# Channel shuffle in place: eight buffers of 24 KB a partition, or four of 48 KB

## The chip, the cores and the metric

One core of a Trainium2 chip. The metric is the device time of one execution in microseconds: 317.66 us before the change, the median of three runs (317.65 to 317.87). A profiled execution gives the trace that is read here.

## The reference

The tensor x has 16 x 64 x 64 positions of 256 channels in float32. The channels of each position are read as 8 groups of 32 and written in the order 32 times 8: a transpose of an 8 x 32 block within each position.

```python
x = x.reshape(batch, h, w, groups, channels_per_group)
x = x.transpose(0, 1, 2, 4, 3)
x = x.reshape(batch, h, w, c)
```

Nothing is computed; 67.1 MB are read and 67.1 MB are written.

## The kernel before, in words

The 65,536 positions (rows of 1 KB) are cut into tiles of 128 x q rows. `_SIZES` (line 12) lists q for each tile: twenty tiles of 24, one of 8, one of 24. Each partition holds q consecutive rows, so a tile with q = 24 is 24 KB a partition and 3 MB in all, and both its load and its store move one contiguous run of 24 KB a partition.

For each tile in turn (line 48), a buffer is taken from a pool of eight (line 49), one DMA loads the tile on SP's queue (line 50), and then pieces of 8 rows (1 MB, 8 KB a partition) are shuffled: VectorE (DVE) copies the piece into one of two PSUM buffers named bounce, reading it with the 8 and 32 exchanged (line 54), and ScalarE (ACT) copies it back to where it came from (line 58). After its last piece the tile is stored by one DMA on ACT's queue (line 59). A buffer is free for its next load when its store has landed.

The order of the work is the order in which the program is written: `manual_schedule` keeps each engine's instructions in that order, so a store on ACT that has to wait also holds the copies that ACT does behind it, and with two bounce buffers DVE stops two pieces later. All DMAs, loads and stores together, use eight semaphores in turn; a DMA is not issued before the last DMA that used its semaphore has landed.

Of the kernel before, what the change touches and what calls it, by code (L numbers as in the profile page):

```python
# [1 line left out]

# [4 lines left out]


F32 = mybir.dt.float32
P = 128  # L10

_SIZES = [24] * 20 + [8, 24]
_BUFS = 8

_PIECE = 8


@with_exitstack
def kernel(
    ctx: ExitStack,  # L20
    tc: tile.TileContext,
    x: bass.AP,
    groups: bass.AP,
    out: bass.AP,
):
    nc = tc.nc
    b, h, w, c = x.shape
    G = int(groups)
    CPG = c // G
    assert G * CPG == c  # L30
    assert sum(_SIZES) * P == b * h * w
    biggest = max(_SIZES)

    x_flat = x.rearrange("b h w c -> (b h w c)")
    out_flat = out.rearrange("b h w c -> (b h w c)")

    pool = ctx.enter_context(tc.tile_pool(name="pool", bufs=_BUFS))
    psum = ctx.enter_context(
        tc.tile_pool(name="psum", bufs=2, space=bass.MemoryType.PSUM)
    )  # L40

    def rows(flat, first, q):

        return flat[first * c : (first + P * q) * c].rearrange("(p f) -> p f", p=P)

    ctx.enter_context(tc.manual_schedule(engines=None))
    first = 0
    for q in _SIZES:
        buf = pool.tile([P, biggest * c], F32, name="buf")
        nc.sync.dma_start(out=buf[:, : q * c], in_=rows(x_flat, first, q))  # L50
        for k in range(0, q, _PIECE):
            piece = buf[:, k * c : (k + _PIECE) * c]
            bounce = psum.tile([P, _PIECE * c], F32, name="bounce")
            nc.vector.tensor_copy(  # L54
                out=bounce.rearrange("p (i j g) -> p i j g", j=CPG, g=G),
                in_=piece.rearrange("p (i g j) -> p i j g", g=G, j=CPG),
            )
            nc.scalar.copy(out=piece, in_=bounce)  # L58
        nc.scalar.dma_start(out=rows(out_flat, first, q), in_=buf[:, : q * c])  # L59
        first += P * q  # L60


# [1 line left out]
_INS = ['x', 'groups']  # L64
_OUTS = [((16, 64, 64, 256), 'float32')]

_NUMBERS = {'groups': 8}


# [26 lines left out]
```

## Time and profile before

| | |
|---|---|
| median of three runs | 317.66 us |
| the profiled execution's own time | 317.64 us |
| its span | 315.9 us |
| DVE, 64 copies | 227.9 us busy, 3636 ns each |
| ACT, 64 copies back | 119.0 us busy, 1866 ns each |
| load of 3 MB, median from issue to landing | 58.4 us |
| store of 3 MB, median from issue to landing | 24.2 us |
| HBM read and written | 67.11 MB each, 425 GB/s over the span |

Times from issue to landing hold the time that a DMA stands in the queue behind others. The rows of the profile name an instruction by its line, engine, operation and tiles. Times in the timeline and in the chain of waits are microseconds from the start of the span. "DMA share" is the busy share of the 16 DMA engines, on which the queues of SP (q1) and ACT (q10) both run.

### The profile page before, as it was taken

To read this page: it belongs to the slowest core of one execution; us is meant where nothing else is said; L and a number is where in the kernel's file an instruction comes from. 1 tells how busy PE (TensorE), PEld (TensorE's weight loads), DVE (VectorE), ACT (ScalarE), POOL (GpSimd) and SP (SyncE) were. 2 spreads that over 40 slices of the span, in tenths; PEclk is the share of its full clock that TensorE was granted. 3 is DMA by queue.
4 is the path that set the end of the run, shared out by engine and by line. 5 is a ranking of instruction groups with operands and counts; after the bars stand their busy time and mean duration, and the time that the engine had idled before them with its cause. 6 is when DMAs were issued, how large, how long until landed. Compare 5 with 4: busy or idle time off the path is not lost.

```text
span 315.9 us, 289 instructions
## 1 busy us (share of the span) xinstructions
DVE 227.9 (72%) x64; ACT 120.3 (38%) x65; POOL 0.2 (0%) x4
## 2 busy tenths in 40 slices
DVE  0699999959587685957008986999970299999900
ACT  0354455525252424330015416545500444555420
POOL 0000000000000000000000000000000000000000
DMA  8999999999999999999999999999999999999997
GB/s 296 439 442 380 436 429 433 433 439 433 423 442 433 426 442 426 426 442 426 433 436 427 433 436 436 433 426 437 433 423 448 423 429 444 429 423 433 439 432 302
DMA packets 6338, 134.24 MB, mean 425 GB/s; under 512 B 704, under 2 KB 704, under 8 KB 704
## 3 DMA queue, kind: packets, MB, share of 16 engines
q1 hardware_dynamic: 3168, 67.11, 49.9%
q10 hardware_dynamic: 3168, 67.11, 49.4%
q14 instruction: 2, 0.02, 0.0%
HBM read 67.11 MB, written 67.11 MB: 425 GB/s over the span
## 4 chain that ended last, share of the span: by engine, by line
DVE 54%; another core or an unknown queue 23%; issue 8%; ACT 5%; DMA 3%; DVEq 1%; ACTq 0%
DVE bounce L54 54%; ACT buf L58 5%; DMA buf<-in_x_dram 3%; DVEq L91 1%; ACTq L59 0%; DVEq L54 0%; ACTq L58 0%
## 5 line engine op out<-in xcount | busy, mean ns | idle before, releaser
L54 DVE COPY bounce<-buf 128x2048 f32<-128x2048 f32 x64 | 227.9, 3636 | 72.6 <-ACT buf L58 38.8
L58 ACT COPY buf<-bounce 128x2048 f32<-128x2048 f32 x64 | 119.0, 1866 | 171.1 <-DVE bounce L54 115.3
L58 ACT ACT_TABLE_LOAD x1 | 1.3, 1283 | 11.1 <-DMA buf<-in_x_dram 11.1
L77 POOL MEMSET const-bfloat16-1.0<- 128x1 bf16 x1 | 0.1, 102 | 0.0
L77 POOL MEMSET const-uint8-127<- 128x1 uint8 x1 | 0.1, 101 | 0.0
L77 POOL MEMSET const-float32-0.0<- 128x1 f32 x1 | 0.1, 99 | 0.2 <-issue 0.2
L77 POOL MEMSET const-float32-1.0<- 128x1 f32 x1 | 0.1, 98 | 0.0
## 6 DMA issues: line engine op xcount, KB each, us to landing
buf<-in_x_dram SPq DMA_DIRECT2D x21, 3072.0 KB, 58.4
out_dram<-buf ACTq DMA_DIRECT2D x21, 3072.0 KB, 24.2
buf<-in_x_dram SPq DMA_DIRECT2D x1, 1024.0 KB, 46.0
out_dram<-buf ACTq DMA_DIRECT2D x1, 1024.0 KB, 15.8
```

The lines of the kernel that those rows point to most:

```text
L54: nc.vector.tensor_copy(out=bounce.rearrange("p (i j g) -> p i j g", j=CPG, g=G), in_=piece.rearrange("p (i g j) -> p i j g", g=G, j=CPG),)
L58: nc.scalar.copy(out=piece, in_=bounce)
L77: nc = _bacc.Bacc("TRN2", target_bir_lowering=False, num_devices=1)
L91: with _tile.TileContext(nc) as tc:
```

## The change

The tiles become one of 8, one of 24 and ten of 48, in this order, and the pool has four buffers of 48 KB a partition, as much memory as eight of 24 KB. A tile of 48 is loaded by two DMAs of 24 KB a partition each, both issued before its shuffle. Its pieces are shuffled as before, the first half's first. It is stored by one DMA of 48 KB a partition after its last piece; the last three tiles are stored by two DMAs, each half after its own third piece. Seven tiles of 48 are thus stored whole.

```diff
-_SIZES = [24] * 20 + [8, 24]
-_BUFS = 8
+_SIZES = [8, 24] + [48] * 10
+_BUFS = 4
+
+_LOAD = 24
+
+_HALVED = 3
...
-    for q in _SIZES:
+    for t, q in enumerate(_SIZES):
         buf = pool.tile([P, biggest * c], F32, name="buf")
-        nc.sync.dma_start(out=buf[:, : q * c], in_=rows(x_flat, first, q))
-        for k in range(0, q, _PIECE):
-            piece = buf[:, k * c : (k + _PIECE) * c]
...
-            nc.scalar.copy(out=piece, in_=bounce)
-        nc.scalar.dma_start(out=rows(out_flat, first, q), in_=buf[:, : q * c])
+        src, dst = rows(x_flat, first, q), rows(out_flat, first, q)
+        whole = t < len(_SIZES) - _HALVED
+        for a in range(0, q, _LOAD):
+            cols = slice(a * c, min(a + _LOAD, q) * c)
+            nc.sync.dma_start(out=buf[:, cols], in_=src[:, cols])
+        for a in range(0, q, _LOAD):
+            b = min(a + _LOAD, q)
+            for k in range(a, b, _PIECE):
+                piece = buf[:, k * c : (k + _PIECE) * c]
...
+                nc.scalar.copy(out=piece, in_=bounce)
+            if whole and b == q:
+                nc.scalar.dma_start(out=dst, in_=buf[:, : q * c])
+            elif not whole:
+                cols = slice(a * c, b * c)
+                nc.scalar.dma_start(out=dst[:, cols], in_=buf[:, cols])
         first += P * q
```

Below, tiles are counted from 0, and "a" and "b" are the first and second half of a tile of 48 (tile 9's second half is 9b).

More of the change, by code (lines that the diff above doesn't have):

```diff
@@ L26 @@
     nc = tc.nc
-    b, h, w, c = x.shape
+    n, h, w, c = x.shape
     G = int(groups)
@@ L30 @@
     assert G * CPG == c
-    assert sum(_SIZES) * P == b * h * w
+    assert sum(_SIZES) * P == n * h * w
     biggest = max(_SIZES)
@@ L47 @@
     first = 0
-    for q in _SIZES:
+    for t, q in enumerate(_SIZES):
         buf = pool.tile([P, biggest * c], F32, name="buf")
-        nc.sync.dma_start(out=buf[:, : q * c], in_=rows(x_flat, first, q))
-        for k in range(0, q, _PIECE):
-            piece = buf[:, k * c : (k + _PIECE) * c]
[L53 to L59, printed above, removed]
+        src, dst = rows(x_flat, first, q), rows(out_flat, first, q)
[7 more added lines that the diff above has]
+                piece = buf[:, k * c : (k + _PIECE) * c]
+                bounce = psum.tile([P, _PIECE * c], F32, name="bounce")
+                nc.vector.tensor_copy(
+                    out=bounce.rearrange("p (i j g) -> p i j g", j=CPG, g=G),
+                    in_=piece.rearrange("p (i g j) -> p i j g", g=G, j=CPG),
+                )
+                nc.scalar.copy(out=piece, in_=bounce)
[4 more added lines that the diff above has]
+                nc.scalar.dma_start(out=dst[:, cols], in_=buf[:, cols])
         first += P * q
```

## The prediction

> **What bounds the kernel.** I read the page's header and slices first, then windows, then the chain of waits, then the end of the timeline. The header and the DMA rows of the page:
>
> ```profile
> span 315.9 us, 289 instructions
> DVE 227.9 (72%) x64; ACT 120.3 (38%) x65; POOL 0.2 (0%) x4
> ...
> DMA  8999999999999999999999999999999999999997
> ...
> q1 hardware_dynamic: 3168, 67.11, 49.9%
> q10 hardware_dynamic: 3168, 67.11, 49.4%
> ```
>
> No engine is busy beyond 72%; the 16 DMA engines are full in every slice but the first and last, half of it for loads (q1), half for stores (q10). Windows (columns: window, length, three engines, clock, DMA share, GB/s) show that nothing is left between the ends:
>
> ```profile
> 0.00:12.00 12.00, 0.95 (x1) 0.90 (x1) 0.20 (x4) 1.00 0.89 348
> 12.00:300.00 288.00, 226.41 (x64) 117.50 (x64) 0.00 (x0) 1.00 1.00 431
> 300.00:316.00 16.00, 0.53 (x1) 1.86 (x1) 0.00 (x0) 1.00 0.84 362
> ```
>
> So the time is bytes over rate plus the ends. In the trace's packet records a 24 KB partition row is one packet of 0.912 us, eight per DMA engine for each transfer of 3 MB (7.3 us). I count in pieces of 8 rows, 1 MB: 0.912 x 8 / 3 = 2.43 us each. Moving 64 pieces in and 64 out takes 128 x 2.43 = 311.3 us. Lines of the timeline (start, length, engine, line, operation) give the end:
>
> ```profile
> 67.99 10.70 DVE L54 COPY bounce<-buf 128x2048 f32<-128x2048 f32 x3 [3.61 <-DMA buf<-in_x_dram]
> ...
> 80.62 0.34 ACTq L59 DMA_DIRECT2D out_dram<-buf  x1
> ...
> 302.46 0.34 ACTq L59 DMA_DIRECT2D out_dram<-buf  x1
> ```
>
> The last store is issued at 302.46 and lands 12.4 us later (the tile's shortest time to landing), at 314.9; the span ends 1.0 us after. So 314.9 - 311.3 = 3.6 us is the start: dispatch, and first packets of 1.3 to 2.3 us. The same lines give the compute latency: a tile's load landed at 67.99, its store was issued at 80.62, so 12.6 us for three pieces. Before the end this latency is covered, because the store queue holds other stores: the last load lands at 287, when 52.5 pieces are stored (3.6 + (64 + 52.5) x 2.43 = 287), and the remaining 11.5 keep the DMA engines busy for 28 us.
>
> The chain of waits has one more fact:
>
> ```profile
> 136.89 1.86 ACT buf L58
> 138.75 25.46 another core or an unknown queue
> 164.21 0.02 issue
> ```
>
> A store ready at 138.75 waits 25 us although its data are ready. The compiled order shows why: the DMAs use eight semaphores in turn, and this store's was last used by the load of tile 12, which lands at that moment. The loads filled the DMA engines meanwhile, so it cost nothing.
>
> **What the skill says.** The Trainium skill, "DMA: Bandwidth & Descriptors", section "Queues, rings and completion order": each DMA engine goes round-robin between the rings with work, at packet granularity, a whole packet before it switches. The trace agrees, and shows that a turn is a packet whatever its size: the one 1 MB load, with 8 KB rows beside stores of 24 KB rows, needs 9.7 us, which is 8 x (0.31 + 0.91), not the 4.9 us of an equal share by bytes. Same page, "Where 436 GB/s comes from": ceiling 435 GB/s; the trace runs at 431, so nothing is to be had from the rate. Same page, "Rules for kernel authors": transfers of at least 1 MiB, coalesced. All of these are above it: 8 KB rows take 0.309 us and 24 KB rows 0.912, so the fixed part is (3 x 0.309 - 0.912) / 2 = 0.008 us a packet.
>
> **The change part by part.** *Instructions.* DVE and ACT keep their 64 copies each, in the same forms. Loads stay 22; stores go from 22 to 15. Seven issues of 0.34 us leave ACT, hidden behind the DMA engines. Bytes are the same. Seven stores of 6 MB save 7 x 8 x 0.008 = 0.4 us of DMA time at most. *The small tile first.* It lets DVE start about 5 us earlier (1 MB loads 4.9 us sooner than 3 MB). Worth 0: in this stretch loads already fill the engines. *Four buffers of 48.* The same rows in flight. A load waits for the store of a whole 6 MB tile, but several loads are queued ahead (below). *48 KB rows.* The trace of before has none. If a row stays one packet, it takes 2 x 0.912 = 1.82 us a turn against 0.91 for a load's, so a store takes two thirds of the DMA engines: stores catch up with loads, and loads finish later. From below the effect is 0, where a row counts as two packets. I take one packet, since 8 and 24 KB rows each were one. *What then happens.* Stores of tiles 6, 7 and 8 carry the shared-semaphore wait: the compiled order makes the store of tile 8 wait for the first load of tile 9, and so on. So:
>
> Store 8 is issued when tile 9's first half has landed: 46 + 3 pieces in; 40 out (store 7 is done). That is 3.6 + 89 x 2.43 = 220. Check: store 7 was issued likewise at 3.6 + (43 + 34) x 2.43 = 191, needs 4.0 us to its first packet under load (first store of before: issued 23.68, first packet 27.7) and 8 x (1.82 + 0.91) = 21.9, so lands at 217; and tile 8 was loaded near 203, so computed at 216. Both precede 220. Behind the waiting store stand ACT's copies of tile 9, and behind them, two pieces on, DVE; but tile 9's data land at the same 220, so the wait holds up nothing else. Store 8 runs from 224 to 246. In the 4.0 us loads alone move 1.65 pieces, and in the 21.9 us eight more packets, 3 pieces: at 246, 53.6 in, 46 out. Then all stores are halves and alternate with loads one to one. Are there always stores? Halves 9a and 9b are computed by 246; 10a and 10b (loaded near 253 and 267) by 266 and 280, before 9a and 9b (29 us) and then 10a are through. Yes. So the last 10.4 pieces in go with 10.4 out: the last load lands at 246 + 20.8 x 2.43 = 296.5, with 56.4 stored, not 52.5. Left are 1.6 pieces of tile 10 and 3 of 11a, 11 us, while the last half needs 12.6 us of compute. Its store is issued at 296.5 + 12.6 = 309.1, and with nothing ahead of it takes 7.3 us of packets plus issue and landing. A lone store is not in the trace. Below: 7.3 + 1.1 (first load: issue 0.73, first packet 1.8) = 8.4. Above: the first load's 10.3, cold packets included. I take 8.7, with 0.3 for landing. End 317.8, against 314.9: +2.9, less up to 0.4 for fewer packets: **+2.5**. The profiled execution of before, 317.64 (span 315.9), is the median within 0.02, so 317.66 + 2.5 = **320.1 us**. One packet of phase either way, 0.9 us, at each of two hand-overs, with the lone store's bounds, makes +0.7 to +4.5.
>
> The halving of the last three tiles is inside this sum: with whole stores there, the last would be 6 MB and 7.3 us longer.
>
> **The rivals.**
> *A, no change (not slower).* 48 KB rows are served as two packets of 24 KB, or turns go by bytes. Then the queues alternate evenly, the loads keep their lead, and the last load lands before 314.9 - 12.6 - 8.7 = 293.6, the point from which it decides: the DMA engines never run dry, and the end is 314.9 less at most 0.4. For it: the lead of 11.5 pieces before. Against: the turn by packet in the 1 MB load. Time 317.3 to 317.8.
> *B, a hole in the middle.* Loads run out, since a buffer comes free only when 6 MB have been stored. The price would be up to 12.6 + 4.0 us a round for some rounds; one such round makes 334. Against: at 217, when store 7 frees its buffer, the half-tiles 9a to 10b are still queued, 3 to 4 x 7.3 us of work.
> *C, faster.* Larger packets move quicker than the fixed 0.008 us says, by 2 us over 44 MB. Nothing in the profile speaks for it: the share is 1.00 at 431 GB/s. Near 315.5.
>
> **How the numbers follow.** What this kernel's measurement can tell from no change is about 0.2%, 0.6 us. Chances: main 0.70, A 0.23, B 0.04, C 0.03. Of the main case 0.02 falls under 0.6 us of loss; so slower 0.72, same 0.25, faster 0.03. Range: the main case's own is 318.4 to 322.2. A holds 0.23, too much to leave out, so low is 317.2; high 321.8 leaves out B and the main case's top.
>
> **What would show it.** Right: one DMA hole of 2 to 4 us near 307 to 311, in slices that are full before; the last DVE piece at about 303 to 307 instead of 297; the last store issued near 309, about 9 us before its landing; 6 MB stores with 48 KB packets of 1.8 us, one per turn. Stores of tiles 6 to 8 issued some us after their last copy. Wrong: a load queue that ends before 293, no hole at the end, or packets of 24 KB on the store queue (A); DMA share below 0.98 between 30 and 290 (B). The weakest step is the phase between stores and loads at 246.

## The result and the profile after

The changed kernel takes 333.83 us, the median of four executions (327.97 to 337.76), against 317.65 (317.57 to 317.87) beside it: the ratio is 1.040, with a 95% interval of 1.027 to 1.052. Here and below a ratio leaves out executions more than 1.5% above the fastest of the same kernel, so it can stand below the quotient of the medians. 320.1 was forecast, with a range up to 321.8. The direction and the kind of loss were as forecast. The size was not: 2.5 us were forecast, and the ratio makes it 12.6, five times as much. A second thing stands out: the four executions of before lie within 0.3 us of each other, those of after within 10.

The profiled execution took 327.97 us, with a span of 326.2, so 10.3 us of span, four times the forecast, are to be explained. From the page of the changed kernel (busy time, two rows of the span in 40 slices, packets and megabytes of the two queues):

```profile
span 326.2 us, 266 instructions
DVE 228.4 (70%) x64; ACT 120.7 (37%) x65; POOL 0.2 (0%) x4
...
DMA  8999999999999999999999999999999999997936
...
q1 hardware_dynamic: 3168, 67.11, 48.4%
q10 hardware_dynamic: 2160, 67.11, 48.2%
```

DVE's and ACT's copies cost what they cost before, and the bytes are the same. The row of DMA slices is full up to the 36th and then reads 7, 9, 3, 6, where before it was full up to the last slice, which read 7. The store queue has 2160 packets instead of 3168. That is 896 of 48 KB, 896 of 24 KB, 128 of 8 KB and 240 very short ones that close the stores: a row of 48 KB is one packet. In the packet records it takes 1.815 us (median), against 0.912 for 24 KB.

Windows of the changed kernel (window, length, busy time of three engines, clock, DMA share, GB/s):

```profile
12.00:165.00 153.00, 121.27 (x35) 61.58 (x33) 0.00 (x0) 1.00 1.00 431
165.00:298.00 133.00, 91.46 (x27) 48.52 (x26) 0.00 (x0) 1.00 1.00 426
298.00:303.00 5.00, 1.34 (x1) 1.87 (x1) 0.00 (x0) 1.00 0.47 202
303.00:309.00 6.00, 5.54 (x2) 1.87 (x1) 0.00 (x0) 1.00 1.05 451
309.00:317.00 8.00, 5.16 (x2) 3.73 (x2) 0.00 (x0) 1.00 0.22 92
317.00:327.00 10.00, 0.00 (x0) 0.00 (x0) 0.00 (x0) 1.00 0.68 290
```

There are two holes, at 298 to 303 and at 309 to 317. Even in them the share isn't 0: some of the 16 DMA engines work on while others have nothing. The second hole is what the timeline shows of the last tile (start, length, engine, line, operation, and the idle time before with what ended it):

```profile
303.46 10.70 DVE L64 COPY bounce<-buf 128x2048 f32<-128x2048 f32 x3 [4.11 <-DMA buf<-in_x_dram]
...
316.08 0.34 ACTq L73 DMA_DIRECT2D out_dram<-buf  x1
```

The last half tile has landed at 303.4, its three pieces take 12.7 us to the issue of the store at 316.08, and the store needs 9.1 us to its landing at 325.2. The kernel ends 1.0 us later.

Now the 16 DMA engines one by one. For each of the 37 DMAs of the changed kernel the trace has 16 increments of the DMA's semaphore with their times, one from each DMA engine whose share has landed. Below, "ends" are these 16 times of one DMA. In the kernel before, the ends of the last load lie between 285.2 and 287.0. In the changed kernel the first is at 292.5 and the last at 303.4; the mean of the 16 is 295.5. Load by load, the sixteen ends lie within 0.5 us until tile 7's first half (161 us), but for one early load with 1.2. The second halves of tiles 7, 8 and 9 have 2.1, 5.2 and 10.2, and the last load 10.9.

The packet records show where DMA engines have nothing to do. Most of them stand idle from 298.5 to 302.3 and from 309.6 to 317.0, 11.2 us together. The slowest is never idle: its last three stores land at 310.6, 317.9 and 325.2, 7.3 us apart, which is the time of eight packets.

So the last DMA engine decides. 303.4 + 12.7 + 9.1 is the end, and on the fastest engine the same load was there at 292.5, before the 293.6 from which the prediction's rival A counts no hole. On this one engine two chains end together: the late load with its compute, and its own packets without a gap.

What made some engines late is also in the records: single packets that take longer than their kind's median. A 48 KB packet of a store takes up to 3.0 us instead of 1.82, on a few engines at a time. After the first 40 us of the span such excess sums to 38.0 us over the 16 engines, where the kernel before has 0.9.

### The profile page after: what moved, and what is told of

Same layout as the page of the kernel before. It is cut to its first block, busy times and chain, and to the rows that moved or that the text cites. A ratio compares the mean times of both kernels' runs of the same rounds, so it can differ in the third digit from the quotient of the medians.

```text
span 326.2 us, 266 instructions
## 1 busy us (share of the span) xinstructions
DVE 228.4 (70%) x64; ACT 120.7 (37%) x65; POOL 0.2 (0%) x4
## 3 DMA queue, kind: packets, MB, share of 16 engines
q1 hardware_dynamic: 3168, 67.11, 48.4%
q10 hardware_dynamic: 2160, 67.11, 48.2%
## 4 chain that ended last, share of the span: by engine, by line
DVE 57%; another core or an unknown queue 23%; DMA 13%; issue 2%; DVEq 1%; ACT 1%; SPq 1%
DVE bounce L64 57%; DMA buf<-in_x_dram 13%; DVEq L105 1%; ACT buf L68 1%; SPq L58 1%; DVEq L64 0%
```

## The experiments

Four theories stand in the expectations. T: a store whose packets are larger than the loads' takes more than half of the DMA engines, and that is the cause. K: packets of 48 KB are bad as such. S: rows that lie 48 KB apart in HBM are bad. G: stores of 6 MB, issued in lumps and freeing buffers in lumps, put the DMA engines out of step. T is first taken as the same loss on all 16 DMA engines, 320 us each time; by the last runs it stands for unequal turns as the cause, whatever their path to the time. The kernel before was measured beside every run, with medians of 317.6 to 317.7.

### All tiles in halves

```diff
-_HALVED = 3
+_HALVED = 12
```

> The changed kernel with every tile of 48 stored in halves of 24 KB rows, so no packet is above 24 KB; buffers of 48 KB and rows 48 KB apart in HBM stay. Theory T (turns: a 48 KB packet gets a whole turn, stores overtake the loads, the last load is late): 317.3 to 318.0 us, no hole at the end. Theory K (48 KB packets, beyond their turns, put the 16 DMA engines out of step): the same. Theory S (rows 48 KB apart in HBM make store packets slow on some DMA engines): still above 322 us, with 24 KB store packets of 1.3 us in the second half.

Measured: 317.62 us (317.43 to 317.94), ratio 0.9999 (0.999 to 1.0007). Windows of this run:

```profile
12.00:300.00 288.00, 224.34 (x63) 115.30 (x62) 0.00 (x0) 1.00 1.01 431
300.00:316.00 16.00, 0.21 (x1) 1.87 (x1) 0.00 (x0) 1.00 0.84 361
```

This is the end of the kernel before, almost to the number (0.84 and 362 there). Four buffers of 48 KB, the order of the tiles and two loads a tile cost nothing; all of the loss belongs to the whole stores. S falls too, since these rows lie 48 KB apart as well.

### A 6 MB store of 24 KB packets

```diff
-        return flat[first * c : (first + P * q) * c].rearrange("(p f) -> p f", p=P)
+        m = min(q, _LOAD)
+        return flat[first * c : (first + P * q) * c].rearrange(
+            "(t p f) -> p t f", p=P, f=m * c
+        )
```

A tile of 48 is two blocks in HBM, each with 24 KB a partition, so its one store has 16 packets of 24 KB for each DMA engine instead of 8 of 48.

> The changed kernel with each tile of 48 laid out as two blocks of 24 KB a partition in HBM; the whole store is still one DMA of 6 MB, but of 16 packets of 24 KB on each DMA engine. Theories T, K and S: 317.3 to 318.0 us. Only if the 6 MB store or the four buffers as such cost time (theory G, granularity) is it above 320 us.

Measured: 322.5 us (318.19 to 323.5), ratio 1.0108 (1.0037 to 1.0178). This is less than a third of the loss, but it isn't nothing, and T, K and S all asked for nothing; only G had said above 320. In its profiled execution, the slowest of the four, the loads' ends drift from 1.9 to 8.6 us apart and the excess of slow packets sums to 55.3 us, in bursts near 160 and 225 us. Packets are equal here. So unequal turns are not the only thing that puts DMA engines out of step; what does it here stays open.

### Rows 48 KB apart, in the kernel before

```diff
-    def rows(flat, first, q):
+    def rows(flat, first, q, t):
+        if t < 20:
+            lo = first - P * q * (t % 2)
+            pair = flat[lo * c : (lo + 2 * P * q) * c].rearrange("(p f) -> p f", p=P)
+            return pair[:, (t % 2) * q * c : (t % 2 + 1) * q * c]
```

> The kernel before, its eight buffers and 3 MB transfers kept, with two neighbouring tiles interleaved so that their 24 KB rows lie 48 KB apart in HBM. Theories T and K: as the kernel before, 317.4 to 317.9 us. Theory S: above 320 us, with store packets of 24 KB that take 1.3 us on some DMA engines.

Measured: 318.00 us (317.77 to 318.32), ratio 1.001 (1.0003 to 1.0016): 0.4 us for all of it. S falls for the second time.

### Loads of 48 KB, stores of 24 KB

```diff
-        for a in range(0, q, _LOAD):
-            cols = slice(a * c, min(a + _LOAD, q) * c)
+        step = q if whole else _LOAD
+        for a in range(0, q, step):
+            cols = slice(a * c, min(a + step, q) * c)
...
-            if whole and b == q:
+            if False:
...
-            elif not whole:
+            else:
```

> The changed kernel the other way round: tiles of 48 loaded by one DMA of 48 KB rows (the last three in halves), all stored in halves of 24 KB rows. Theory T: now loads get two thirds, the last load lands before 290, no hole at the end, 317.3 to 318.5 us. Theory K: 48 KB packets again, so DMA engines out of step by up to 10 us in the second half and above 320 us. Theory S: above 320 us.

Measured: 318.21 us (317.67 to 318.88), ratio 1.0018 (1.0012 to 1.0025). The same packets of 48 KB, on the other queue, cost a twentieth of the loss; the loads' ends stay within 1.8 us and the stores' within 2.7. K falls.

### The changed kernel again, and three ways to move its whole stores

> The changed kernel itself, for a second trace beside the others. Theory T (the turn of 48 KB alone: stores overtake loads, the same on all 16 DMA engines) gives the same 320 us each time. Theory G (the DMA engines get out of step, so that each transfer lands with its slowest engine): 326 to 338 us, varying by several us from run to run, the last load landing 5 to 12 us later on its slowest engine than on its fastest.

Measured, with no edit: 332.31 us (326.97 to 339.3); the last load's ends lie between 290.5 and 307.6, and slow packets sum to 108.9 us. The effect and its scatter are there again, and T as the same loss on all DMA engines falls: it asked for 320 us each time.

Loads of tiles 2 to 8 also in 48 KB rows:

```diff
-        for a in range(0, q, _LOAD):
-            cols = slice(a * c, min(a + _LOAD, q) * c)
+        step = q if whole else _LOAD
+        for a in range(0, q, step):
+            cols = slice(a * c, min(a + step, q) * c)
```

> The changed kernel with tiles of 48 (but the last three) also loaded by one DMA of 48 KB rows, so that loads and stores have equal turns. Theory T: nobody is overtaken, 317.3 to 318.5 us. Theory G (it is the 6 MB store: between two of them the store queue is empty, and the DMA engines start again unevenly): above 320 us, with a spread of 4 us or more between engines.

Measured: 325.47 us (321.82 to 326.92), ratio 1.0205 (1.0145 to 1.0265). That is what G had said, not T. The records show why the edit did not test T: the stores of tiles 7 and 8, 48 KB rows, run at 198 to 246 us beside loads that are 24 KB again. Up to the last 48 KB load (194 us) the loads' ends stay within 2.2 us and loads lead by up to 14 pieces; from 198 to 242 the lead falls from 12.7 to 6.8 pieces, and the last load's ends lie at 295.7 to 301.1. Of 22.5 us of slow packets, 18.5 begin between 200 and 260. Windows of this run:

```profile
12.00:299.00 287.00, 213.80 (x60) 111.72 (x60) 0.00 (x0) 1.00 1.00 429
...
307.00:315.00 8.00, 4.91 (x2) 3.73 (x2) 0.00 (x0) 1.00 0.16 68
```

That explanation came after the run, so it is put to the test below.

Whole stores early only, then only late:

```diff
-_HALVED = 3
+_HALVED = 6
```

> The changed kernel with the last six tiles of 48 stored in halves instead of the last three: only tiles 2 to 5 are stored whole. In the changed kernel's trace the DMA engines are in step to within 0.5 us up to here. Theory G: spread at the end below 3 us, 317.3 to 319 us. Theory T: the stores have caught up with the loads by tile 5 and stay close behind them, so the hole at the end stays: 319.5 to 322 us.

```diff
-        whole = t < len(_SIZES) - _HALVED
+        whole = 6 <= t < len(_SIZES) - _HALVED
```

> The other way round: tiles 2 to 5 stored in halves, tiles 6 to 8 whole, the last three in halves. Theory T: the loads keep their early lead but lose it over three whole stores; 318 to 320 us, the same in every run. Theory G: the engines get out of step from tile 6 on, 320 to 335 us, varying from run to run.

Measured: 326.14 us (323.62 to 332.48), ratio 1.0238 (1.0195 to 1.0281), and 328.89 (324.83 to 330.25), ratio 1.0308 (1.024 to 1.0377). With whole stores early, the loads' ends come apart by 6.3 us at 94 to 100 us and by 17.1 at 158, shortly before the last whole store lands (166). Then all rows are 24 KB. The gap falls to 8.6 us at 200, grows again to 17.6 at 226, and then stays at 17.7 for five loads, to 298, with a DMA share of 1.00 in that stretch. With whole stores late, the ends lie within 2.5 us until 159, then up to 3.9, 8.0 and 17.4 us apart, and 11.5 at the last load. So the gap starts where whole stores run, and it isn't made up by the end, though its cause ended 130 us before. That it grew again among rows of 24 KB is not explained. The first of these two missed T's numbers as well as G's, and the second fits G's, not T's; T's times were too low, since it had no term for DMA engines out of step.

### Two stores of 3 MB, back to back

```diff
             if whole and b == q:
-                nc.scalar.dma_start(out=dst, in_=buf[:, : q * c])
+                for d in range(0, q, _LOAD):
+                    cols = slice(d * c, min(d + _LOAD, q) * c)
+                    nc.scalar.dma_start(out=dst[:, cols], in_=buf[:, cols])
```

> The changed kernel with each whole 6 MB store replaced by two stores of 3 MB (24 KB rows) issued one after the other at the same place, after the tile's last copy: buffers come free at the same points of the program, and the store queue gets its work in the same lumps. Theory T (turns): equal turns, no overtaking, 317.3 to 319 us. Theory G, if it is the lumps and not the size of one DMA: above 320 us, with engines out of step by 4 us or more. If it is the single 6 MB DMA: 317.3 to 319 us as T.

Measured: 317.73 us (317.44 to 317.97), ratio 1.0004 (0.9995 to 1.0013), the loads' ends within 2 us. Here 6 MB become ready at once, go out in one lump and free the buffer in one lump, but in 24 KB packets. So lumps cost nothing; of G only the single store of 6 MB is left.

### Both at 48 KB, and never unequal

Like the run with both at 48 KB, but tiles 7 and 8 are stored in halves, so that no 48 KB store meets 24 KB loads:

```diff
+        joined = t < len(_SIZES) - _HALVED - 2
...
-            if whole and b == q:
+            if joined and b == q:
...
-            elif not whole:
+            elif not joined:
```

> As the kernel with 48 KB rows on both sides, but tiles 7 and 8 also stored in halves, so that 48 KB stores never run beside 24 KB loads. Theory T: the lead of 13 pieces that the loads have at tile 6 is kept to the end, the last load lands before 290, no hole at the end: 317.3 to 319 us although five tiles are stored by 6 MB DMAs. Theory G: still 320 us or more.

Measured: 317.19 us (316.59 to 318.86), ratio 0.9988 (0.9979 to 0.9997). Windows of this run:

```profile
12.00:300.00 288.00, 224.35 (x63) 117.36 (x63) 0.00 (x0) 1.00 1.00 432
300.00:315.00 15.00, 0.00 (x0) 0.00 (x0) 0.00 (x0) 1.00 0.86 369
```

Five stores of 6 MB with 48 KB rows remain, and the ends lie within 1.0 us, slow packets at 2.2 us. Against the run with both at 48 KB only the stores of tiles 7 and 8 are split, and 8 us go. So G falls, and the explanation of the miss holds: neither 6 MB nor packets of 48 KB are enough to make a store harmful; here it takes smaller packets in the loads beside it. The 6 MB store of 24 KB packets, with its 1.1%, stays an exception. These two runs also speak against a rival, that the DMA engines restart unevenly after the store queue has run dry. By the packet records it runs dry in both for about 1 us at 84, 113, 142 and 171 us, with under 2 us of slow packets from 60 to 200; in the run with both at 48 KB it does not run dry between 175 and 300, where the slow packets are. This is also the one version that is ahead of the kernel before, by 0.1%, which its 4608 packets instead of 6336 would fit; it is less than the 0.2% that the prediction took as what can be told.

### The kernel before, with loads of 12 KB rows

The sharpest test leaves tiles, buffers, DMAs, bytes and stores as they were before and makes the loads' packets smaller. Each load reads two blocks of 12 KB a partition:

```diff
-        nc.sync.dma_start(out=buf[:, : q * c], in_=rows(x_flat, first, q))
+        nc.sync.dma_start(
+            out=buf[:, : q * c].rearrange("p (t f) -> p t f", t=2),
+            in_=x_flat[first * c : (first + P * q) * c].rearrange(
+                "(t p f) -> p t f", t=2, p=P
+            ),
+        )
```

> The kernel before with nothing changed but the rows of the loads: each load of 3 MB is still one DMA, but reads two blocks of 12 KB a partition, so it has 16 packets of 12 KB on each DMA engine and a store 8 of 24 KB (rows land at other places of the tile, so the output's rows are in another order; the work is the same). Theory T: stores get two thirds, the lead falls to its floor, the last load lands at about 294 to 299, and a hole of 4 to 7 us opens after 307: 321 to 325 us. Theory G (only 6 MB stores harm): 317.4 to 318.5 us.

Measured: 334.12 us (331.05 to 335.9), ratio 1.0501 (1.0433 to 1.057). The DMA slices and the two queues on the page of this run:

```profile
DMA  7999999999999999999999999999999999999217
...
q1 hardware_dynamic: 5984, 67.11, 48.2%
q10 hardware_dynamic: 3168, 67.11, 47.2%
```

The loads are 5984 packets now, beside 3168 of the stores. Windows of this run:

```profile
165.00:308.00 143.00, 103.20 (x29) 57.45 (x31) 0.00 (x0) 1.00 1.01 427
308.00:324.00 16.00, 10.71 (x3) 5.60 (x3) 0.00 (x0) 1.00 0.15 64
324.00:333.00 9.00, 0.00 (x0) 0.00 (x0) 0.00 (x0) 1.00 0.77 328
```

The last tile in its timeline:

```profile
310.46 10.71 DVE L59 COPY bounce<-buf 128x2048 f32<-128x2048 f32 x3 [11.96 <-DMA buf<-in_x_dram]
...
323.10 0.34 ACTq L64 DMA_DIRECT2D out_dram<-buf  x1
```

The same picture as in the changed kernel, without any 6 MB or 48 KB in it: DMA engines full until the last load, one hole, one lone store. The last load's ends lie between 291.4 and 310.4, and again 12.7 us lie between its landing and the store, which lands after 8.7 us. The mean of the 16 is 298.5. A load landing then would end the span at 298.5 + 12.7 + 8.7 + 1.0 = 320.9, 5.0 us later than before; the other 11.9 us of the 16.9 are the last engine's distance from the mean. T had the direction, and its last load at 294 to 299 is right as a mean; its 321 to 325 us again lacked the last engine.

Two things changed with that edit, though: the turns, and the two blocks that a load reads. The last two runs part them.

### Both in 12 KB rows, and the stores alone

Both directions in two blocks of 12 KB a partition, the addresses of the run before and equal turns again:

```diff
-        nc.scalar.dma_start(out=rows(out_flat, first, q), in_=buf[:, : q * c])
+        nc.scalar.dma_start(
+            out=out_flat[first * c : (first + P * q) * c].rearrange(
+                "(t p f) -> p t f", t=2, p=P
+            ),
+            in_=buf[:, : q * c].rearrange("p (t f) -> p t f", t=2),
+        )
```

> The kernel before with loads and stores both moved as two blocks of 12 KB a partition: the same addresses for the loads as in the kernel with 12 KB loads alone, but equal turns again. Theory T (unequal turns do the harm): 317.6 to 319.5 us, the small rest being twice as many packets; spread between engines below 3 us. If alternating between two blocks in HBM is what slowed the packets there: above 325 us still.

Measured: 319.32 us (319.27 to 319.48), ratio 1.0054 (1.0037 to 1.0071), ends within 1.6 us. One window of this run:

```profile
12.00:300.00 288.00, 225.58 (x64) 117.52 (x64) 0.00 (x0) 1.00 1.01 429
```

No hole. A packet of 12 KB takes 0.460 us, so two take 0.008 us more than one of 24 KB. With 336 such pairs on each DMA engine that is at most 2.7 us; 1.6 were lost of span. So the price of more packets is enough to cover it.

With this store and the loads of before, the turns are unequal the other way round (the rows of the output stand in another order, as in the run with the loads alone):

> The kernel before with the stores alone moved as two blocks of 12 KB a partition, loads in rows of 24 KB: unequal turns the other way. Theory T: loads get two thirds and gain on the stores, the last load lands before 287, no hole at the end: 317.6 to 319.5 us. If unequal turns of either sign put the engines out of step and that alone costs the time: above 322 us.

Measured: 318.49 us (318.34 to 318.59), ratio 1.0026 (1.0016 to 1.0035), half of the price above for half of the extra packets. The timeline's last instruction:

```profile
284.85 0.38 ACTq L59 DMA_DIRECT2D out_dram<-buf  x1
```

The loads, which carry 66% of the bytes at 60 to 100 us, end at 270 instead of 287, the last store is issued at 284.85 instead of 302.46, and stores alone fill the rest. The blocks in HBM are harmless in the loads and in the stores; smaller packets in the loads than in the stores are not. Unequal turns of either sign, which asked for more than 322 us, fall.

## Why the prediction was wrong

**Right: what bounds the kernel, and what a turn is.** DMA engines full between the ends; a row of 48 KB one packet, at 1.815 us where 1.82 was worked out. The Trainium skill, "DMA: Bandwidth & Descriptors", section "Queues, rings and completion order", has each DMA engine drain a whole packet before it switches. It does not say that a partition row is a packet; here the records show that. The prediction's reading of it, that larger rows take a larger share, is shown by the packet records. The loads' share of the bytes is 50% in the kernel before (60 to 120 us), 32% in the changed kernel while a store of 48 KB rows runs (57 to 70 us), 33% with loads of 12 KB rows (40 to 60 us) and 66% with stores of 12 KB rows. Rival A needed turns by bytes or two packets a row, and fell. B fell: no hole between 12 and 298. C fell.

**Right: the waits.** The store of tile 8 was to wait for the load of tile 9 until about 220. The timeline of the changed kernel:

```profile
221.76 0.34 ACTq L70 DMA_DIRECT2D out_dram<-buf  x1
222.19 10.70 DVE L64 COPY bounce<-buf 128x2048 f32<-128x2048 f32 x3 [5.00 <-DMA buf<-in_x_dram]
```

Its last copy had ended at 219.1, so it waited 2.7 us, and tile 9's first piece starts right behind it, because both waited for the same load. As forecast, the wait held up nothing. At 246 us, where the prediction has 53.6 pieces in and 46 out and saw its weakest step, 54.0 and 45.5 had been moved.

**Right: the two terms of the end.** The compute of the last half took 12.7 us, where 12.6 was taken. A lone store takes 8.7 us, as was taken: so it is in the changed kernel run again, with both at 48 KB and with loads of 12 KB rows. In the changed kernel's own trace it took 9.1, because on the slowest DMA engine the store before it landed only at 317.9; on the other engines it landed after 8.5 to 8.7. The hole was to be at 307 to 311 and one; it was in two parts, and longer.

**Wrong: the landing of the last load.** The step is the sentence that puts it at 296.5: 246 + 20.8 pieces of 2.43 us. It treats 16 DMA engines as one, in step all the way. As a mean it was right within 1.0 us: the 16 ends average 295.5. With all 16 there, the end would have been 295.5 + 12.7 + 8.7 + 1.0 = 317.9 of span, 2.0 more than before, close to the 2.5 forecast; this is an estimate, since the mean itself could be another one without slow packets. But the load landed with its last engine, at 303.4. These 7.9 us by which the last is behind the mean, and 0.4 by which the last store was late on the same engine, are the difference between 317.9 and the profiled span, 326.2. The skill's same page, section "Why a DMA increments its semaphore by 16 and not by 1", says that a DMA's 16 engines finish independently and that the semaphore counts them; the trace of before had hidden what that can mean, with its loads' ends at most 2.0 us apart. So the range was too narrow by a term that it did not have.

The 7.9 us have the same cause in the main, the unequal turns. In the same tiles, the loads' ends stay within 2 us when all stores are halves, when they are pairs of halves, and, at 6 MB, when the loads have 48 KB rows too; and the kernel before, given loads of 12 KB rows, comes apart by 19 us. They are also what varies: in the second profiled execution of the changed kernel the last load landed 4.2 us later than in the first (307.6 against 303.4), and the execution took 3.8 us more (331.81 against 327.97).

**What stays open.** Why single packets become slow when the stores' are the larger ones: the runs show that they do, not by what. Kernels with larger packets in the stores have 22 to 109 us of it, those with equal packets 0.9 to 2.2, those with larger packets in the loads 0.9 (24 KB over 12) and 15 (48 over 24, nearly all in one burst at 95 to 105 us). Unequal rows need not be there at that moment: in the changed kernel 14 of the 38 us come after the last 48 KB packet (253 us). The exception is the 6 MB store of 24 KB packets: equal packets, 55 us, and 1.1%. Nor does the lag follow from the excess by a rule: the last DMA engine of the changed kernel had 11 us less idle time than most, and its load came 11 us later; with 12 KB loads 7 us less idle time went with 19 us. One reading is that the stores, issued for all engines at the same moment, take their share first and leave the whole deficit to the loads. The run with whole stores early looks like it: its five stores that land from 219 to 278 end within 1.3 us on the 16 engines, while the loads beside them are 17.7 us apart. It was not tried by an experiment.

## What to carry to other kernels

Where loads and stores keep the DMA engines full, give both the same row size, or the loads the larger one: in this kernel 24 KB stores over 12 KB loads cost 5.0%, the reverse 0.3%. Equal rows are no guarantee, since stores of 6 MB in 24 KB rows still cost 1.1%. When the last load is late, this kernel ends with that load on its slowest DMA engine, then that tile's compute, then a store alone. Bytes over rate give the mean of the 16 engines; the last one was 4 to 12 us behind it here where the stores had the larger rows, and the trace of before, with 2 us, did not show that. Where a change makes a store larger, look at what the loads beside it then do.

## What the runs showed of the hardware that was not expected

- DMA engines of one core came 10 to 22 us apart in their loads, and one gap of 17.7 us stayed from 226 to 298 us, 60 us and more after the last 48 KB store had landed.
- With a load and a store in both queues a turn was one partition row: rows of 48 KB beside 24 left the smaller ones 32% of the bytes, rows of 24 KB beside 12 left them 33%.
- A kernel with the same DMAs, bytes and buffers takes 5.0% longer when only its loads' rows go from 24 to 12 KB, and 0.5% when its stores' rows do so too.
- A contiguous partition row was one packet at every size here: 8 KB 0.309 us, 12 KB 0.460, 24 KB 0.912, 48 KB 1.815, which is about 0.008 us a packet beside the bytes.
- A store of 3 MB with nothing ahead of it took 8.7 us from issue to landing, in three runs, 7.3 of it packets.
